# All sums of gated values and of down weights on VectorE, and twelve load tiles in the FFN stages of a hybrid decoder layer

## The chip, the cores and the metric

The kernel runs on one core of a Trainium2 chip. Its engines are TensorE (PE, with its weight loads shown apart as PEld), VectorE (DVE), ScalarE (ACT), GpSimd (POOL) and SyncE (SP). In this kernel SP issues the transfers between the chip's main memory and the on-chip tiles. The metric is the time of one execution on the device in microseconds (us); the median of several runs is compared.

## The reference, cut to what matters

One layer of a decoder trunk over 2048 tokens of width 1024, in fp32:

```python
u = rmsnorm(h, attn_pre_norm); proj = u @ w_in
o_hg = rmsnorm(hgrn2_mix(...)) * silu(hg)          # gated linear recurrence, 4 heads
o_sb = rmsnorm(stick_breaking_mix(sq, sk, sv))     # attention, 8 heads of width 64
h = h + rmsnorm(concat(o_hg, o_sb) @ w_out, attn_post_norm)
u = rmsnorm(h, ffn_pre_norm)
gate, up = split(u @ w_gate_up, 2816)              # w_gate_up: 1024 x 5632
y = (silu(gate) * up) @ w_down                     # w_down: 2816 x 1024
h = h + rmsnorm(y, ffn_post_norm)
out = h + (p @ ple_proj) * sigmoid(h @ ple_gate)   # ple_gate: 1024 x 1024
```

The change concerns the third block, the FFN: the products with w_gate_up and w_down and what lies between them.

## The kernel before

**Products.** Every fp32 product is made of three matmuls on rounded parts (function mm3, lines 223 to 225): an operand is split into a high part, a copy that ACT makes (line 811), and a low part, operand minus high part, which DVE or POOL computes (line 812, in pair_of). Tiles are 128 x 512 fp32 values, 256 KB.

**Seven products instead of eight.** The FFN and the PLE gate multiply 2 x 2 blocks by the scheme of Strassen and Winograd: seven products, in the order CHAIN = (1, 2, 6, 3, 7, 5, 4), of blocks and of sums of blocks. Each product's result leaves PSUM through DVE or ACT in the function chain, which adds it to the others (lines 816 and 819 are the helpers sub and add; line 926 is ACT's copy of the first product).

**Stages.** The tokens stand in four groups of 512, taken two at a time. After attention and the output projection come six stages, put in a row by the class Drive: gate_up(0), down(0), gate_up(1), down(1), ple(0), ple(1). gate_up has 11 blocks of the 2816 columns, seven steps each. A step has two parts: prepare, which loads and splits its weights, and run, which issues its 24 matmuls (two banks of 12 each). Drive calls prepare three steps ahead of run in a gate_up stage, four ahead in a down stage and five in a ple stage.

**Between gate/up and down.** When a block's last product is done, run applies the gate (sigmoid on ACT, line 996; products on DVE, lines 997 and 998) and holds four quarters of gated values: h11, h12, h21, h22. down needs seven operands of them: h11, h12, h22 and the four sums s1 to s4. They are computed in tiles named hs (lines 1013, 1014, 1018, 1019) and stored to hid_s in main memory (lines 1016 and 1021); down loads them back from there. The hs tiles come from a pool "acc" that the gate's sg tiles and the transposer's results share.

**Sums of down weights.** down also needs four sums of the w_down blocks for each of its 11 column blocks k. down_combos(k) loads four blocks, forms four sums in place (b_combos, four instructions of line 816) and stores them to wd_s (line 834). It is called while gate_up(0) runs, once every six steps from step 12 on. Even k have their sums on DVE, odd k on POOL. ple_combos does the same for the PLE gate's weights during gate_up(1).

**Other work in gate_up(0).** Also hung on its steps: the operands of its later products (t_second, four loads of u_s for each k), the late normalization of the last token group (post_late: DVE line 715, POOL line 716, ACT line 718) and the transposition of two groups (turn: loads at line 730, transposes on TensorE at line 745, copies on ACT at line 751, stores at line 752).

**Load tiles.** All these loads (function load, line 796) and the transposer's go into tiles named wr, of which there are WR = 10; a load can start when the instructions that read the tile's last contents are done. SP issues loads and stores in one queue, in order.

**Order.** TensorE's instructions stand in the order of the program (manual_schedule for PE alone). Those of the other engines and of SP are put in order by a planner that simulates the program's time; changing an instruction's engine can change its place and that of others. Each engine then executes its queue in order.

Of the kernel before, what the change touches and what calls it, by code (L numbers as in the profile page):

```python
# [25 lines left out]
DFF = 2816  # L26
PLE = 256
EPS = 1e-6
WR = 10
LEVELS = (1, 2, 4, 8, 16, 32, 64)  # L30
BL = 32

# [56 lines left out]
def hybrid_block(  # L89
# [89 lines left out]
    def mm_bank():  # L179
        mm_count[0] += 1  # L180
        return bank(mm_tags[mm_count[0] % len(mm_tags)])
# [8 lines left out]
    def xt(name="xt"):  # L190
        return fb.tile([P, GT], F32, tag="xt", name=name, bufs=8)
# [30 lines left out]
    def mm3(o, l, r, start, stop):  # L222
        nc.tensor.matmul(o, l[0], r[0], start=start, stop=False)  # L223
        nc.tensor.matmul(o, l[0], r[1], start=False, stop=False)  # L224
        nc.tensor.matmul(o, l[1], r[0], start=False, stop=stop)  # L225
# [559 lines left out]

    SLOTS = {"u": (12, 16), "w": (4, 4), "wr": (WR, 0), "acc": (2, 4)}
    big = [None, None]
# [6 lines left out]
    def load(src, shape=None):  # L794
        r = slot("wr", 0, "wr")
        nc.sync.dma_start(r if shape is None else shape(r), src)
        return r

    def acc(name="acc"):
        turns["acc"] += 1  # L800
        return slot("acc", 0 if turns["acc"] % 3 == 0 else 1, name)

    def pair_of(src, kind, prod, lo_engine):
        if kind == "u":
            side = 0 if prod in (1, 2, 6) else 1
        else:
            turns["w"] += 1
            side = turns["w"] % 2
        hi = slot(kind + "h", side, kind + "h", F32R)
        lo = slot(kind + "l", side, kind + "l", F32R)  # L810
        nc.scalar.copy(hi, src)  # L811
        lo_engine.tensor_tensor(lo, src, hi.bitcast(F32), op=ALU.subtract)  # L812
        return hi, lo

    def sub(e, o, a, b):
        e.tensor_tensor(o, a, b, op=ALU.subtract)

    def add(e, o, a, b):
        e.tensor_tensor(o, a, b, op=ALU.add)  # L819

    V, G = nc.vector, nc.gpsimd

    def b_combos(b11, b12, b21, b22, e):

        sub(e, b11, b12, b11)
        sub(e, b12, b22, b12)
        sub(e, b22, b22, b11)
        sub(e, b21, b22, b21)

    def combos(blk, dst, e):  # L830
        t = [load(blk(i, j)) for i, j in ((0, 0), (0, 1), (1, 0), (1, 1))]
        b_combos(*t, e)
        for i, r in zip((1, 3, 4, 2), t):
            nc.sync.dma_start(dst[i - 1], r)

    wd_s = [dram.tile([4, P, GT], F32, tag=f"wd_s{k}", name=f"wd_s{k}") for k in range(DFF // 256)]
    wp_s = [dram.tile([4, P, GT], F32, tag=f"wp_s{k}", name=f"wp_s{k}") for k in range(ND // 2)]

    def down_combos(k):
        def blk(i, j):  # L840
            r = (2 * k + i) * P
            return w_down[r:r + P, j * GT:(j + 1) * GT]

        combos(blk, wd_s[k], G if k % 2 else V)

    def ple_combos(k):
        def blk(i, j):
# [74 lines left out]
    def chain(prod, c, b, new):  # L922

        if prod == 1:
            c["u"] = new("cu")
            nc.scalar.copy(c["u"], b)
        elif prod == 2:
            c[1, 1] = new("c11")
            add(V, c[1, 1], b, c["u"])
        elif prod == 6:  # L930
            add(V, c["u"], b, c["u"])
        elif prod == 3:
            c[1, 2] = new("c12")
            add(V, c[1, 2], b, c["u"])
        elif prod == 7:
            add(V, c["u"], b, c["u"])
        elif prod == 5:
            add(V, c[1, 2], b, c[1, 2])
            c[2, 2] = new("c22")
            add(V, c[2, 2], b, c["u"])  # L940
        else:
            c[2, 1] = c["u"]
            sub(V, c[2, 1], c["u"], b)
# [9 lines left out]
    def gate_up(grp, tt):  # L953
        def block(fb):
            s = {}
            cs = [{}, {}]

            def wload(i, j):
                out = []
                for n in range(2):  # L960
                    r = slice((4 * j + 2 * n) * P, (4 * j + 2 * n + 2) * P)
                    c0 = i * DFF + fb * 256
                    out.append(load(w_gate_up[r, c0:c0 + 256].rearrange("(k p) n -> p k n", p=P),
                                    lambda r: r.rearrange("p (k n) -> p k n", k=2)))
                return out

            def prepare(prod):
                if prod == 1:
                    w = wload(0, 0)
                elif prod == 2:  # L970
                    w = wload(0, 1)
                elif prod == 6:
                    w, a21, a22 = wload(0, 0), wload(1, 0), wload(1, 1)
                    s["s1"] = [xt("s1") for _ in range(2)]
                    s["s3"] = [xt("s3") for _ in range(2)]
                    for n in range(2):
                        add(V, s["s1"][n], a21[n], a22[n])
                        sub(V, s["s3"][n], w[n], a21[n])
                        sub(V, w[n], s["s1"][n], w[n])
                    s["s2"] = w  # L980
                elif prod == 3:
                    w = wload(0, 1)
                    for n in range(2):
                        sub(V, w[n], w[n], s["s2"][n])
                elif prod == 7:
                    w = s["s3"]
                elif prod == 5:
                    w = s["s1"]
                else:
                    w = wload(1, 1)  # L990
                s[prod] = [pair_of(t, "w", prod, V if n or prod in (6, 3) else G) for n, t in enumerate(w)]

            def gated(j):
                for q in range(2):
                    sg = acc("sg")
                    nc.scalar.activation(sg, cs[q][1, j], AF.Sigmoid)
                    nc.vector.tensor_tensor(sg, cs[q][1, j], sg, op=ALU.mult)
                    nc.vector.tensor_tensor(cs[q][2, j], cs[q][2, j], sg, op=ALU.mult)

            def run(prod):  # L1000
                for q in range(2):
                    b = mm_bank()
                    for k in range(ND // 2):
                        o = (k % 2) * 256 + q * P
                        mm3(b, [t[:, o:o + P] for t in s[prod][k // 2]], tt[prod, k], k == 0, k == ND // 2 - 1)
                    chain(prod, cs[q], b, new_gu)
                if prod == 5:
                    gated(2)
                if prod == 4:
                    gated(1)  # L1010
                    h11, h12, h21, h22 = cs[0][2, 1], cs[1][2, 1], cs[0][2, 2], cs[1][2, 2]
                    s1, s3 = acc("hs"), acc("hs")
                    add(G, s1, h21, h22)
                    sub(G, s3, h11, h21)
                    for i, t in ((1, h11), (2, h12), (4, h22), (5, s1), (7, s3)):
                        nc.sync.dma_start(hid_s[grp][fb, i - 1], t)
                    s2, s4 = acc("hs"), acc("hs")
                    sub(G, s2, s1, h11)
                    sub(G, s4, h12, s2)
                    for i, t in ((6, s2), (3, s4)):  # L1020
                        nc.sync.dma_start(hid_s[grp][fb, i - 1], t)

            return {prod: (lambda p=prod: prepare(p), lambda p=prod: run(p)) for prod in CHAIN}

        blocks = [block(fb) for fb in range(DFF // 256)]
        steps = []
        if grp == 0:
            for part in (CHAIN[:3], CHAIN[3:]):
                for b in blocks[:2]:
                    steps += [b[p] for p in part]  # L1030
            blocks = blocks[2:]
        return steps + [b[p] for b in blocks for p in CHAIN]
# [269 lines left out]
    for k in range(DFF // 256):  # L1302
        at(0, 12 + 6 * k - (k > 9), lambda k=k: down_combos(k))
# [45 lines left out]
```

## Time and profile before

| | |
|---|---|
| median of 3 runs | 3080.39 us (3078.42 to 3082.84) |
| profiled execution | 3079.93 us, of it 3078.1 us in the span of the profile |
| TensorE busy | 2928.8 us, 95% of the span |
| DVE, POOL, ACT busy | 2042.8, 1603.7, 1580.6 us |
| mean granted TensorE clock | 0.987 |
| transfers | 602.29 MB, mean 196 GB/s |

Times in the rows shown below count from the start of the span. A row of an instruction has its start, its duration, the engine, the line, the operation, the tiles written and read with their shapes, the count, and in brackets the idle time of the engine before it and what ended that idle time. A row of a wait names who waited for whom, then the total in us, the number of waits and the longest. Matmuls overlap, so the distance from one start to the next says more than a duration. The granted clock is given as a share of full speed.

### The profile page before, as it was taken

Reading aid. Unit: us, or ns where it says so; the run is one execution under the profiler, and the core shown is the slowest. Engines: PE = TensorE matmul, PEld = TensorE weight load, DVE = VectorE, ACT = ScalarE, POOL = GpSimd, SP = SyncE. Lnnn points to the kernel's source line nnn. Section 1 sums busy time; section 2 is a strip of 40 time slices with the busy share of each in tenths; the row PEclk is TensorE's granted clock in tenths of the full one; section 3 lists DMA queues with packets and bytes.
Section 4 is the critical chain, followed back from the end, with each engine's and each line's share of the span. In section 5 each row is a group of like instructions: output and inputs, shape, how many; then the busy total and the mean of one; then the engine's idle time right before and its main releaser. Section 6 shows DMA issues by size and latency. Waiting matters only on the chain. (4 is left out here: it accounts for less than half of the span.)

```text
span 3078.1 us, 52969 instructions
## 1 busy us (share of the span) xinstructions
PE 2928.8 (95%) x18280; PEld 2429.9 (79%) x18280; DVE 2042.8 (66%) x2809; ACT 1580.6 (51%) x3188; POOL 1603.7 (52%) x1598
## 2 busy tenths in 40 slices
PE   8999999999999998888998999999899999999989
PEld 7888787878787877778776877788788888887767
DVE  3556566677767776745877766856687766656674
ACT  5666656666667666757523233445432323545442
POOL 3344455545556666857454544645634343556564
PEclk9999999999999999999999999999999999999999
DMA  7765565555444443457767767766955555677874
GB/s 216 217 211 164 157 185 158 148 156 162 141 140 150 147 144 122 164 176 264 253 212 245 238 214 236 234 198 218 328 179 171 172 170 175 209 225 251 286 246 144
DMA packets 469421, 602.29 MB, mean 196 GB/s; under 512 B 43168, under 2 KB 277664, under 8 KB 469152
## 3 DMA queue, kind: packets, MB, share of 16 engines
q1 hardware_dynamic: 469152, 598.91, 61.4%
q8 instruction: 144, 2.36, 0.3%
q14 instruction: 125, 1.02, 0.1%
HBM read 439.89 MB, written 158.86 MB: 195 GB/s over the span
## 5 line engine op out<-in xcount | busy, mean ns | idle before, releaser
L811 ACT CAST wh<-wr 128x512 fp32r<-128x512 f32 x600 | 352.3, 618 | 511.1 <-PE mm L224 139.0
L812 POOL TENSOR_TENSOR wl<-wr,wh 128x512 fp32r<-128x512 f32 x256 | 368.7, 1447 | 386.3 <-ACT wh L811 366.8
L435 POOL TENSOR_TENSOR a<-be,ring 128x512 f32<-128x512 f32 (+2 forms) x320 | 318.4, 995 | 434.5 <-DVE ring L431 418.3
L223 PE MATMUL mm<-uh,wh 128*128 128x512 f32 x1168 | 484.5, 415 | 5.2 <-DVE vv L350 3.2
L225 PE MATMUL mm<-uh,wl 128*128 128x512 f32 x1168 | 460.6, 394 | 0.0
L224 PE MATMUL mm<-ul,wh 128*128 128x512 f32 x1168 | 459.0, 393 | 1.6 <-DVE ul L812 1.6
L812 DVE TENSOR_TENSOR wl<-wr,wh 128x512 fp32r<-128x512 f32 x344 | 308.9, 902 | 204.4 <-ACT wh L811 177.6
L431 DVE TENSOR_TENSOR_SCAN ring<-z,ring,be 128x512 f32<-128x512 f32 x192 | 245.6, 1279 | 113.4 <-ACT z L417 110.0
L223 PE MATMUL mm<-wh,uh 128*128 128x256 f32 (+1 forms) x992 | 308.6, 311 | 0.0
L224 PE MATMUL mm<-wl,uh 128*128 128x256 f32 (+1 forms) x992 | 293.4, 296 | 1.6 <-DVE wl L812 1.3
L225 PE MATMUL mm<-wh,ul 128*128 128x256 f32 (+1 forms) x992 | 292.9, 295 | 0.0
L225 PEld LDWEIGHTS mm<-uh,wl 128*128 128x128 f32 x1168 | 220.5, 189 | 51.0
L223 PEld LDWEIGHTS mm<-uh,wh 128*128 128x128 f32 x1168 | 221.4, 190 | 47.6 <-issue 3.3
L224 PEld LDWEIGHTS mm<-ul,wh 128*128 128x128 f32 x1168 | 221.9, 190 | 41.7 <-DVE ul L812 2.0
L448 DVE TENSOR_TENSOR al<-tr,ah 128x512 fp32r<-128x512 f32 (+1 forms) x320 | 192.0, 600 | 90.1 <-ACT ah L446 89.4
L209 ACT CAST wh<-wr 128x512 fp32r<-128x512 f32 x288 | 178.2, 619 | 135.8 <-PE mm L224 81.5
L210 POOL TENSOR_TENSOR wl<-wr,wh 128x512 fp32r<-128x512 f32 x144 | 189.1, 1313 | 98.2 <-ACT wh L209 95.0
L446 ACT CAST ah<-tr 128x512 fp32r<-128x512 f32 (+1 forms) x320 | 167.6, 524 | 110.1 <-PE tr L443 107.1
L416 ACT ACTIVATE be<-z 128x512 f32<-128x512 f32 (+2 forms) x320 | 171.0, 534 | 90.5 <-PE z L410 38.3
L224 PEld LDWEIGHTS mm<-wl,uh 128*128 128x128 f32 x992 | 191.3, 193 | 8.0 <-DVE wl L812 1.7
L223 PEld LDWEIGHTS mm<-wh,uh 128*128 128x128 f32 x992 | 191.0, 193 | 8.1
L225 PEld LDWEIGHTS mm<-wh,ul 128*128 128x128 f32 x992 | 190.7, 192 | 4.3
(305 smaller groups left out, 7285.6 us busy)
## 6 DMA issues: line engine op xcount, KB each, us to landing
wr<-in_w_gate_up_dram SPq DMA_DIRECT2D x308, 256.0 KB, 3.4
wr<-in_w_in_dram SPq DMA_DIRECT2D x224, 256.0 KB, 3.1
wr<-hid_s SPq DMA_DIRECT2D x154, 256.0 KB, 3.1
wr<-in_w_down_dram SPq DMA_DIRECT2D x110, 256.0 KB, 3.3
hid_s<-hs SPq DMA_DIRECT2D x88, 256.0 KB, 2.7
wr<-wd_s SPq DMA_DIRECT2D x88, 256.0 KB, 3.1
kt<-k_s SPq DMA_DIRECT2D x80, 256.0 KB, 3.1
vt<-v_s SPq DMA_DIRECT2D x80, 256.0 KB, 3.3
```

Source lines behind the costliest of these rows:

```text
L209: nc.scalar.copy(hi, src)
L210: (lo_engine or nc.gpsimd).tensor_tensor(lo, src, hi.bitcast(F32), op=ALU.subtract)
L223: nc.tensor.matmul(o, l[0], r[0], start=start, stop=False)
L224: nc.tensor.matmul(o, l[0], r[1], start=False, stop=False)
L225: nc.tensor.matmul(o, l[1], r[0], start=False, stop=stop)
L416: nc.scalar.activation(be[:, :n], z[:, :n], AF.Sigmoid, scale=0.125)
L431: nc.vector.tensor_tensor_scan(r[:, o:o + n][:, ::-1], z[:, :n][:, ::-1], be[:, :n][:, ::-1], init, op0=ALU.mult, op1=ALU.bypass)
L435: nc.gpsimd.tensor_tensor(a[:, :n], be[:, :n], r[:, o + 1:o + n + 1], op=ALU.mult)
L446: nc.scalar.copy(hi[:, lo_c:], tr[:, lo_c:])
L448: nc.vector.tensor_tensor(lo[:, lo_c:], tr[:, lo_c:], hi[:, lo_c:].bitcast(F32), op=ALU.subtract)
L811: nc.scalar.copy(hi, src)
L812: lo_engine.tensor_tensor(lo, src, hi.bitcast(F32), op=ALU.subtract)
```

## The change

Three things: the four sums of gated values in every gate/up block are DVE's instead of POOL's (88 instructions in the two stages); the four sums of w_down for odd k are DVE's as for even k (20 instructions); and the pool of load tiles of the FFN and PLE stages has 12 tiles instead of ten, 4 KB more in each partition. The PLE gate's sums stay as they are.

```diff
-WR = 10
+WR = 12
...
-        combos(blk, wd_s[k], G if k % 2 else V)
+        combos(blk, wd_s[k], V)
...
                     s1, s3 = acc("hs"), acc("hs")
-                    add(G, s1, h21, h22)
-                    sub(G, s3, h11, h21)
+                    add(V, s1, h21, h22)
+                    sub(V, s3, h11, h21)
                     for i, t in ((1, h11), (2, h12), (4, h22), (5, s1), (7, s3)):
                         nc.sync.dma_start(hid_s[grp][fb, i - 1], t)
                     s2, s4 = acc("hs"), acc("hs")
-                    sub(G, s2, s1, h11)
-                    sub(G, s4, h12, s2)
+                    sub(V, s2, s1, h11)
+                    sub(V, s4, h12, s2)
                     for i, t in ((6, s2), (3, s4)):
                         nc.sync.dma_start(hid_s[grp][fb, i - 1], t)
```

V is VectorE (nc.vector), G is GpSimd (nc.gpsimd).

## The prediction, made before the changed kernel was run

> **What bounds the kernel now.** I read the page first, then busy time by stage, then what TensorE waited for, then the instructions around its longest waits.
>
> ```profile
> span 3078.1 us, 52969 instructions
> ...
> PE 2928.8 (95%) x18280; PEld 2429.9 (79%) x18280; DVE 2042.8 (66%) x2809; ACT 1580.6 (51%) x3188; POOL 1603.7 (52%) x1598
> ```
>
> TensorE is the bound: 95% of the span. No other engine passes 66%, so the change can only move the 5% in which TensorE stands still, and what a low clock adds. The profiled execution took 3079.93 us (its span and 1.8 us around it), the median of the runs is 3080.39; the sum below is made against 3079.9.
>
> The FFN load tiles come into use shortly before 1486 us. Stages from there (columns: stretch and its length, then busy us of each engine, granted clock, share of the DMA engines, GB/s):
>
> ```profile
> 1486.00:1560.00 74.00, 66.51 (x288) 53.57 (x289) 68.06 (x90) 29.93 (x57) 31.58 (x29) 0.93 0.64 208
> 1560.00:1930.00 370.00, 349.06 (x1524) 282.43 (x1523) 259.28 (x367) 116.87 (x221) 170.32 (x119) 0.98 0.69 228
> ...
> 2196.00:2640.00 444.00, 438.36 (x1921) 357.48 (x1922) 330.19 (x444) 144.35 (x245) 179.69 (x120) 0.99 0.58 187
> ...
> 2860.00:3079.00 219.00, 200.02 (x853) 158.70 (x851) 129.96 (x164) 77.60 (x137) 115.31 (x82) 0.97 0.63 216
> ```
>
> The first two rows are the gate/up stage of group 0: TensorE misses 7.5 and 20.9 us of 444. The third is the same stage of group 1, which misses 5.6, at its start. What it waited for, in 1486 to 1930 and then from 1930 on:
>
> ```profile
> PE hg L745 <- ACT acc L751: 19.1, 6, 12.4
> PE av L225 <- DVE wl L812: 4.7, 2, 4.2
> ```
>
> ```profile
> PE z L224 <- POOL wl L812: 4.0, 1, 4.0
> PE tr L225 <- DVE wl L812: 3.9, 1, 3.9
> PE mm L223 <- ACT wh L811: 3.7, 1, 3.7
> ```
>
> Nobody on TensorE waits for a sum that is moved. What the change can do comes indirectly: through when DVE and POOL get to other work, and through when loads start. The longest wait, followed back through the instructions:
>
> ```profile
> 1655.60 0.75 DVE L715 SCALAR_TENSOR_TENSOR wr<-wr,row_scales 128x512 f32<-128x512 f32 x1 [1.31 <-DMA wr<-in_attn_post_norm_dram]
> ...
> 1661.63 6.57 SPq L796 DMA_DIRECT2D wr<-in_w_gate_up_dram  x4
> 1665.88 0.69 DVE L819 TENSOR_TENSOR s<-wr 128x512 f32<-128x512 f32 x1 [3.73 <-DMA wr<-in_w_gate_up_dram]
> ...
> 1677.11 1.41 POOL L816 TENSOR_TENSOR wr<-wr 128x512 f32<-128x512 f32 x1 [16.70 <-DMA wr<-in_w_down_dram]
> 1677.31 1.75 DVE L715 SCALAR_TENSOR_TENSOR wr<-wr,row_scales 128x512 f32<-128x512 f32 x1
> ...
> 1680.15 1.71 POOL L716 TENSOR_TENSOR wr<-wr 128x512 f32<-128x512 f32 x1
> 1680.66 1.75 DVE L998 TENSOR_TENSOR c<-c,sg 128x512 f32<-128x512 f32 x1
> ...
> 1681.89 0.63 ACT L718 ACTIVATE junk<-wr 128x512 bf16<-128x512 f32 x1 [3.44 <-POOL wr L716]
> ...
> 1683.55 0.68 ACT L751 ACTIVATE acc<-hg,g_ffn 128x512 f32<-128x512 f32 x1
> ...
> 1684.28 1.12 PE L745 MATMUL hg<-ident,wr 128*128 128x128 f32 x4 [12.36 <-ACT acc L751]
> ```
>
> (The first row is an earlier L715, alone: 0.75.) Read it upwards: the transpose waits for ACT's copy (L751), which stands behind ACT L718, which waits for POOL L716, which waits for DVE L715 and stood behind a w_down sum (L816) on POOL; L715 stood in a row of DVE work that began only when a gate/up load landed at 1665.9, and SP needed 6.6 us to issue those four loads. Late loads are at the root, with a POOL sum of the kind that is moved in between.
>
> The start of the stage is of the same kind, before any moved sum is due (the first is after 1560):
>
> ```profile
> 1520.94 0.62 ACT L811 CAST uh<-wr 128x512 fp32r<-128x512 f32 x1 [1.86 <-DMA wr<-u_s]
> 1521.01 1.29 DVE L816 TENSOR_TENSOR wr<-wr 128x512 f32<-128x512 f32 x2 [0.76 <-DMA wr<-u_s]
> ...
> 1522.22 1.76 DVE L812 TENSOR_TENSOR wl<-wr,wh 128x512 fp32r<-128x512 f32 x1
> ...
> 1524.03 0.79 PE L225 MATMUL av<-uh,wl 128*128 128x512 f32 x1 [4.18 <-DVE wl L812]
> ```
>
> **The change, part by part.** Rows of the groups that it touches (POOL first, then DVE; last columns: busy, mean ns of one, idle before):
>
> ```profile
> L816 POOL TENSOR_TENSOR wr<-wr 128x512 f32<-128x512 f32 x28 | 39.3, 1403 | 63.2 <-DMA wr<-in_w_down_dram 44.9 <-DVE c L998 11.4 <-DVE wr L816 4.9
> L816 POOL TENSOR_TENSOR hs<-cu,c 128x512 f32<-128x512 f32 x22 | 38.9, 1768 | 23.1 <-DVE cu L998 21.9 <-DMA wr<-in_w_down_dram 1.2
> L819 POOL TENSOR_TENSOR hs<-c,c 128x512 f32<-128x512 f32 x22 | 36.9, 1677 | 133.4 <-DVE c L998 81.2 <-issue 38.1 <-DMA wr<-in_w_gate_up_dram 14.1
> L816 POOL TENSOR_TENSOR hs<-hs,cu 128x512 f32<-128x512 f32 x22 | 36.2, 1646 | 0.2
> ...
> L816 POOL TENSOR_TENSOR hs<-cu,hs 128x512 f32<-128x512 f32 x22 | 32.3, 1469 | 1.1 <-PE av L225 0.7
> ```
>
> ```profile
> L812 DVE TENSOR_TENSOR wl<-wr,wh 128x512 fp32r<-128x512 f32 x342 | 306.2, 900 | 204.4 <-ACT wh L811 177.6 <-DMA wr<-hid_s 16.7 <-PE z L224 5.2
> ...
> L998 DVE TENSOR_TENSOR cu<-cu,sg 128x512 f32<-128x512 f32 x44 | 49.5, 1130 | 0.1
> ```
>
> Moved: 88 gated sums (4 in each of 22 blocks) and 20 sums of w_down (5 odd k of 4; the other 8 of the 28 are the PLE gate's and stay). POOL loses 38.9 + 36.9 + 36.2 + 32.3 + 20 x 1.403 = 172 us. DVE gains 108 x 0.69 (the s<-wr instruction at 1665.88, alone) = 74.5 us.
>
> But POOL's sums stretch DVE's: at 1680.66, beside POOL L716, an instruction of this form took 1.75 instead of 0.69. So each moved sum gives DVE back between 0 (nothing beside it) and 1.06 us. The group cu<-cu,sg, which runs as the gated sums begin, has an excess of 0.44 each (19.4 us over 88 sums, 0.22 per sum); wl<-wr,wh has 72 us in all. I take 0.4, since more than one group is stretched by the same sum. Net: 108 x 0.29 = +31 us of DVE.
>
> Is DVE then the bound? In group 0's stage it had 68.1 + 259.3 = 327 of 444; 64 of the sums fall there: 327 + 64 x 0.29 = 346 (78%), without relief 371 (84%). In group 1's: 330 + 44 x 0.29 = 343 (77%), without relief 361 (81%). Both lie under TensorE's busy time, so the moved work costs 0 on the path; TensorE's products hide it. With that cover gone altogether it would cost the whole 74.5 us.
>
> SP issues the same transfers in both kernels. A block's four sums take 6.6 us in a row on POOL (144.3 / 22) and 2.8 on DVE, so the hid_s stores, and the loads queued behind them on SP, can go up to 3.8 us sooner; I count that as a margin, since stores were no wait of TensorE.
>
> **Two more load tiles.** A load starts when a tile is free.
>
> ```profile
> wr<-in_w_gate_up_dram SPq DMA_DIRECT2D x144, 256.0 KB, 3.5
> wr<-in_w_down_dram SPq DMA_DIRECT2D x44, 256.0 KB, 3.4
> ```
>
> In the 444 us these two kinds alone make 188 loads, one per 2.4 us, so two tiles bring a load forward by 0 (where its place in SP's order holds it) to 4.7 us. I take 3, as the waits above begin at a load and other loads share the tiles. What that returns:
>
> - Start of the stage (4.18 and some 1 us of waits, then slow matmuls): 3 us of the wait and 2 of the slow stretch, together 5; bounds 0 and 11 (7.5 missed and 3.5 at half clock).
> - The 12.36 us: 3 for the load, 1.0 for L715 (1.75 against 0.75 alone), 1.1 because POOL L716 no longer stands behind the w_down sum after L715 ended at 1679.06, less 0.7 for a sum that now runs on DVE ahead of it, and 0.6 of the slow stretch: 5; bounds 0 and 14.5.
> - The other five transposes that waited (19.1 - 12.4 = 6.7): 1.5.
> - Start of group 1's stage (3.9 and the slow stretch behind it): 3; bounds 0 and 6.2.
> - PLE, 3.7 + 4.0 behind loads: 2; bounds 0 and 7.7.
>
> Sum 16.5: 3079.9 - 16.5 = 3063.4, forecast **3063**.
>
> The slow stretches, behind the start's wait, the 12.36 and the 3.9:
>
> ```profile
> 1524.00:1531.00 7.00, 6.40 (x14) 4.62 (x15) 7.00 (x8) 4.31 (x8) 4.12 (x3) 0.50 0.54 171
> ...
> 1684.00:1691.00 7.00, 6.72 (x24) 5.52 (x25) 6.51 (x7) 1.15 (x3) 7.00 (x6) 0.70 0.98 334
> ...
> 2199.00:2206.00 7.00, 6.27 (x20) 4.70 (x19) 7.00 (x9) 0.59 (x1) 4.26 (x3) 0.67 0.86 256
> ```
>
> They lose 7 x 0.50 = 3.5, 2.1 and 2.3 us. [...]
>
> **Rivals.**
>
> ```profile
> POOL wr L816 <- DMA wr<-in_w_down_dram: 44.9, 3, 24.8
> ```
>
> ```profile
> 1516.85 0.39 PE L224 MATMUL mm<-ul,wh 128*128 128x512 f32 x1
> 1517.08 0.39 PE L225 MATMUL mm<-uh,wl 128*128 128x512 f32 x1
> ```
>
> *DVE is held at the head of its queue (slower).* The w_down sums on POOL waited for their loads 44.9 us in three waits, the longest 24.8, the one above 16.70, with little behind them there. On DVE the same wait holds the evacuations of PSUM and the splits for the next products. gate_up prepares three products ahead; one takes 24 matmuls, which start 0.23 us apart, 5.5 us. If two of the three are really ready, TensorE runs 11 us without DVE; waits of 24.8 and 16.7 then cost 13.8 + 5.7 = 19.5, and slow stretches of 3.5 and 2.1: 25 us. Less the 5 + 3 + 2 that come elsewhere: 3095. It decides from a wait of about 11 us on DVE ahead of a moved sum. For it: the 1665.88 row, where a 3.73 us wait held all of DVE. Against: DVE already carries the even k's sums, the loads come earlier with 12 tiles, and where the sums stand in DVE's order is planned anew. [...]
>
> *No change.* SP issues in a planned order; if its place in that order, not a tile, holds a load, the lead is 0. The chain through ACT L718 and L751 stays. 3079. For it: no moved sum is waited for by TensorE, and group 1's stage lost nothing after its start with ten tiles.
>
> *All of it goes.* Every miss of group 0's stage (28.4 and 5.6 of slow clock) and of group 1's start (6.2): 3080 - 40 = 3040. Against: the chain of L745 runs through ACT's order, which stays long.
>
> **How the numbers follow.** Forecast 0.48 (its own range 3050 to 3074), all gone 0.12 (3040), no change 0.18 (3079), DVE held 0.22 (3095). About 0.2% (6 us) is what a measurement here tells from no change. Faster 0.48 + 0.12 = 0.60, within 0.2% 0.18, slower 0.22. The range takes in the no-change case and most of the two outer ones: 3038 to 3094.
>
> **What would show it.** Right: no hs sum and no w_down sum on POOL, POOL's busy time down by some 170 us, DVE's up by 20 to 45 and not by 75 (relief), wl<-wr,wh nearer 800 ns than 900; DVE's and ACT's waits for gate/up loads fewer in 1486 to 1930; the 4.18 and 12.36 us waits shorter. Wrong: DVE waiting over 11 us for w_down with TensorE idle behind it; DVE over 90% in a gate/up stage; the same waits at L745 with loads no earlier; or a new wait in the PLE stage, since every queue but TensorE's may be ordered anew.

## The result and the profile after

The changed kernel took 3061.07 us in the median of six runs (3057.24 to 3070.8), the kernel before 3079.4 in six runs beside it (3073.11 to 3082.84): a ratio of 0.9945 with a 95% interval of 0.9927 to 0.9963, so 0.55% faster. The forecast was 3063. The profiled execution took 3057.24 us, 3055.5 of it in the span.

The page of the kernel after, span and busy times:

```profile
span 3055.5 us, 52953 instructions
...
PE 2920.4 (96%) x18280; PEld 2425.4 (79%) x18280; DVE 2065.6 (68%) x2917; ACT 1583.7 (52%) x3188; POOL 1463.9 (48%) x1490
```

TensorE issues the same 18280 matmuls and, busy for 96% of the span, is still the bound. DVE has 108 instructions more and only 22.8 us more of busy time; POOL has 108 fewer and loses 139.8 us.

The stages of the kernel after, with the same columns as before (stretch, length, busy us of PE, PEld, DVE, ACT and POOL, granted clock, DMA share, GB/s):

```profile
1486.00:1560.00 74.00, 69.41 (x304) 56.30 (x303) 68.24 (x93) 31.00 (x59) 34.56 (x29) 0.95 0.69 221
1560.00:1930.00 370.00, 353.67 (x1545) 287.53 (x1545) 296.14 (x440) 123.15 (x227) 98.38 (x65) 0.98 0.73 239
1486.00:1930.00 444.00, 423.08 (x1848) 343.82 (x1847) 364.39 (x532) 154.15 (x286) 132.94 (x93) 0.97 0.72 236
2196.00:2640.00 444.00, 441.75 (x1940) 360.45 (x1939) 332.93 (x488) 151.54 (x258) 125.35 (x76) 1.00 0.58 189
```

In the first 444 us after 1486 TensorE does 36 matmuls more than before (1848 against 288 + 1524 = 1812). At 0.23 us from one start to the next (1516.85 to 1517.08 in the kernel before) that is 8.3 us. DVE is at 364 of 444, 82%.

What TensorE waited for in the kernel after, first in group 0's gate/up stage, then from 1930 on (whom it waited for, total us, times, longest):

```profile
PE hg L745 <- ACT acc L751: 13.1, 2, 10.3
PE av L225 <- DVE wl L812: 4.6, 2, 2.5
PE z L223 <- DVE cu L816: 2.9, 1, 2.9
```

```profile
PE mm L224 <- POOL wl L812: 6.7, 1, 6.7
...
PE mm L225 <- DVE wl L812: 2.2, 2, 1.9
```

The long wait at L745 is 10.3 instead of 12.4, the five smaller ones have become one of 2.8 (13.1 less 10.3), the 3.9 at the start of group 1's stage is gone, and a wait of 6.7 in the PLE stage is new. The wait of 2.9 for a sum of products on DVE was 1.3 before.

TensorE's order is the same in every kernel here, so the i-th matmul of one can be set against the i-th of another. Adding up how much sooner each comes than before gives the gain by place. One execution of each kernel stands behind this table, and the part ahead of the FFN, where nothing is changed, differs by up to 9 us between executions, so the column is shown too:

| us gained against before | ahead of the FFN | gate_up(0) | everything after it |
|---|---|---|---|
| after | 1.7 | 9.2 | 12.0 |
| twelve tiles alone | -8.6 | -5.9 | 7.7 |
| all sums on DVE, ten tiles | -0.3 | 17.8 | 3.1 |

The second and third rows are the first two experiments below. They already show the split: the sums gain in gate_up(0), the tiles lose there and gain later (the profiled execution of the second row is a long one, with a span of 3086.2 us, most of it lost ahead of the FFN). The difference between the first and the third row, 8.6 us less in gate_up(0) and 8.9 more after it, says the same of the tiles. So do the other two pairs of kernels that differ in the tiles alone (with one set of sums moved, below): with twelve tiles they gain 3.6 and 2.7 us less in gate_up(0), and 5.7 and 5.4 more after it.

### The profile page after: what moved, and what is told of

It is laid out like the page before. It is cut to its first block, busy times and chain, and to the rows that moved or that the text cites. A ratio compares the mean times of both kernels' runs of the same rounds, so it can differ in the third digit from the quotient of the medians.

```text
span 3055.5 us, 52953 instructions
## 1 busy us (share of the span) xinstructions
PE 2920.4 (96%) x18280; PEld 2425.4 (79%) x18280; DVE 2065.6 (68%) x2917; ACT 1583.7 (52%) x3188; POOL 1463.9 (48%) x1490
## 4 chain that ended last, share of the span: by engine, by line
PE 41%; DMA 6%; DVE 5%; POOL 3%; issue 3%; ACT 1%; SPq 0%; POOLq 0%; ACTq 0%; DVEq 0%
PE mm L223 6%; PE mm L224 6%; PE mm L225 6%; PE z L225 4%; PE z L223 4%; PE z L224 4%; PE tr L223 2%; PE tr L224 2%; PE tr L225 2%; PE av L225 2%; PE av L224 2%; PE av L223 2%; DMA wr<-in_w_gate_up_dram 1%; DVE wr L816 1%; DMA wr<-in_ffn_post_norm_dram 1%
## 5 line engine op out<-in xcount | busy, mean ns | idle before, releaser
L225 PE MATMUL mm<-uh,wl 128*128 128x512 f32 x1168 | 458.9, 393 | 0.0
L812 DVE TENSOR_TENSOR wl<-wr,wh 128x512 fp32r<-128x512 f32 x344 | 299.2, 877 | 181.8 <-ACT wh L811 166.1
L225 PE MATMUL mm<-wh,ul 128*128 128x256 f32 (+1 forms) x992 | 293.6, 296 | 0.0
L225 PEld LDWEIGHTS mm<-uh,wl 128*128 128x128 f32 x1168 | 219.4, 188 | 50.6
L812 POOL TENSOR_TENSOR wl<-s,wh 128x512 fp32r<-128x512 f32 x44 | 97.0, 2211 | 270.8 <-ACT wh L811 242.0
L224 PEld LDWEIGHTS mm<-wl,uh 128*128 128x128 f32 x992 | 191.9, 193 | 12.2 <-POOL wl L812 7.1
```

## The experiments

Every kernel was timed against the kernel before on the same chip; a ratio below 1 is faster than before. The kernel before was timed anew in each of four groups (3079.4, 3079.78, 3079.62 and 3081.08 us); its first median is shown.

| kernel | load tiles | sums on DVE | median us | ratio, 95% interval |
|---|---|---|---|---|
| before | 10 | none of the moved ones | 3079.4 | 1 |
| e1_tiles | 12 | none | 3075.13 | 0.9983 [0.9972, 0.9994] |
| e5_hs | 10 | gated | 3065.27 | 0.9958 [0.9944, 0.9973] |
| e6_wd | 10 | w_down | 3067.6 | 0.9958 [0.9944, 0.9972] |
| e2_sums | 10 | both | 3061.47 | 0.9941 [0.9925, 0.9957] |
| e3_tiles_hs | 12 | gated | 3057.98 | 0.9926 [0.9912, 0.9941] |
| e4_tiles_wd | 12 | w_down | 3066.2 | 0.9949 [0.9933, 0.9965] |
| after | 12 | both | 3061.07 | 0.9945 [0.9927, 0.9963] |
| e8_late_tiles | 10, then 12 | both | 3062.0 | 0.9934 [0.9917, 0.995] |
| e7_no_hs | 10 | w_down; gated left out | 3058.91 | 0.9931 [0.9915, 0.9948] |
| e9_own_out | 10, two for the transposer | both | 3059.94 | 0.9941 [0.9924, 0.9958] |
| e10_copy_dve | 10 | both | 3068.51 | 0.9961 [0.9946, 0.9976] |
| e11_late_copy | 10, then 12 | both | 3070.92 | 0.9961 [0.9947, 0.9976] |
| e12_after_copy | 12 | both | 3059.34 | 0.993 [0.9915, 0.9944] |

### The two halves of the change

Twelve tiles alone:

```diff
-WR = 10
+WR = 12
```

> Twelve load tiles alone, all sums where they were before. Theory A (the gain of 18 us is loads that start earlier): 3060 to 3068, with the waits of 1840 to 1930 and at the start of group 1's gate/up stage gone or halved as in the changed kernel. Theory B (the gain comes from the sums: DVE no longer stretched by them, and the stores and the acc tiles free sooner): 3075 to 3083, with those waits still there. Theory C (only the planner's new order matters, and any small edit moves the time by some 10 us either way): no relation to the changed kernel's stalls, place by place.

All sums on DVE, ten tiles:

```diff
-        combos(blk, wd_s[k], G if k % 2 else V)
+        combos(blk, wd_s[k], V)
...
-                    add(G, s1, h21, h22)
-                    sub(G, s3, h11, h21)
+                    add(V, s1, h21, h22)
+                    sub(V, s3, h11, h21)
...
-                    sub(G, s2, s1, h11)
-                    sub(G, s4, h12, s2)
+                    sub(V, s2, s1, h11)
+                    sub(V, s4, h12, s2)
```

> All 108 sums on DVE, ten load tiles. Theory A: 3075 to 3083, DVE's busy time up by some 25 us and TensorE's waits as before. Theory B: 3060 to 3068. If the two parts need one another: both this run and the one with the tiles alone stay above 3070.

The tiles alone bring 0.17% (by the ratio 0.0017 x 3079.4 = 5 us); the sums alone bring 0.59% (18 us), as much as the whole change. The intervals are far apart. With ten tiles the sums bring the whole gain. Neither theory of the first expectation holds whole: the time of e1_tiles lies in Theory B's range, but the waits between 1840 and 1930 and at the start of group 1's stage are gone, as Theory A had it.

Twelve tiles alone, in group 0's gate/up stage: busy times of the stage, what TensorE waited for, and the instructions around the two long waits (start, duration, engine, line; the bracket is the idle time before and what ended it):

```profile
1486.00:1930.00 444.00, 411.84 (x1813) 335.80 (x1812) 335.58 (x448) 146.99 (x279) 210.96 (x148) 0.96 0.70 228
```

```profile
PE hg L745 <- ACT acc L751: 19.1, 2, 11.4
PE av L223 <- DVE c L819: 4.7, 1, 4.7
PE z L225 <- DVE wl L812: 3.7, 1, 3.7
```

```profile
1632.28 1.15 ACT L996 ACTIVATE sg<-c 128x512 f32<-128x512 f32 x2 [14.73 <-DVE c L819]
...
1637.81 0.67 ACT L751 ACTIVATE acc<-hg,g_ffn 128x512 f32<-128x512 f32 x1
...
1638.53 1.12 PE L745 MATMUL hg<-ident,wr 128*128 128x128 f32 x4 [7.63 <-ACT acc L751]
...
1696.00 2.35 DVE L998 TENSOR_TENSOR cu<-cu,sg 128x512 f32<-128x512 f32 x2
1697.78 0.69 ACT L751 ACTIVATE acc<-hg,g_ffn 128x512 f32<-128x512 f32 x1 [7.78 <-DVE cu L998]
...
1698.52 1.11 PE L745 MATMUL hg<-ident,wr 128*128 128x128 f32 x4 [11.44 <-ACT acc L751]
```

TensorE is busy for 411.8 us of the window, before for 66.51 + 349.06 = 415.6; this execution reaches the stage some 10 us later, so the window takes in a little more of the work ahead of it. The waits at L745 sum to the same 19.1 us as before, in two instead of six. In the first, ACT's copy L751 stands in ACT's queue behind a sigmoid L996 that itself waited 14.7 us for its operand; in the second it waits 7.8 us for DVE's L998, which reads an sg tile of the pool "acc" and so releases the tile that the copy writes. Neither ends with a load. More of ACT's idle time in this stage now lies ahead of a sigmoid. The row of ACT's waits for it, of before, of twelve tiles alone, and of the changed kernel:

```profile
ACT sg L996 <- DVE c L819: 51.3, 14, 13.7
```

```profile
ACT sg L996 <- DVE c L819: 102.8, 18, 18.4
```

```profile
ACT sg L996 <- DVE c L819: 88.9, 21, 15.8
```

In the five kernels with twelve tiles in this stage it is 79 to 103 us, in eight of the nine with ten 48 to 64. The ninth, e7_no_hs, has 78.1 and the largest gain of all in this stage (24.6 us, table below), so this idle time alone does not make a kernel slow; that ACT's order is what twelve tiles cost here is argued, not shown.

All sums on DVE with ten tiles, the same views:

```profile
1486.00:1930.00 444.00, 430.30 (x1887) 350.60 (x1886) 369.62 (x538) 155.74 (x290) 134.11 (x95) 0.98 0.72 239
```

```profile
PE hg L745 <- ACT acc L751: 7.2, 1, 7.2
PE av L225 <- DVE wl L812: 4.0, 2, 3.4
```

```profile
1661.52 0.69 DVE L819 TENSOR_TENSOR s<-wr 128x512 f32<-128x512 f32 x1 [3.23 <-DMA wr<-in_w_gate_up_dram]
...
1673.68 0.74 DVE L715 SCALAR_TENSOR_TENSOR wr<-wr,row_scales 128x512 f32<-128x512 f32 x1
...
1674.56 1.59 POOL L716 TENSOR_TENSOR wr<-wr 128x512 f32<-128x512 f32 x1 [1.95 <-DVE wr L715]
...
1676.18 0.63 ACT L718 ACTIVATE junk<-wr 128x512 bf16<-128x512 f32 x1 [1.36 <-POOL wr L716]
...
1677.83 0.68 ACT L751 ACTIVATE acc<-hg,g_ffn 128x512 f32<-128x512 f32 x1
...
1678.57 1.11 PE L745 MATMUL hg<-ident,wr 128*128 128x128 f32 x4 [7.18 <-ACT acc L751]
```

This is the chain of before (L715, L716, L718, L751, L745) with the POOL sums taken out of it: L715 takes 0.74 us instead of 1.75, and POOL is idle and waits for L715 instead of standing behind its own work. From L715 to L745 it takes 4.9 us instead of 7.0. That is 2.1 of the 5.7 us by which the transpose comes sooner, less 0.7 because DVE's row from the load to L715 is longer (12.2 us for 11.4). The other 4.4 us come from further up: the row of DVE work still begins when a gate/up load lands, but that is at 1661.5 instead of 1665.9, with no tile more. SP's queue shows where the load was held. Before, and then with all sums on DVE:

```profile
1640.34 3.37 SPq L1021 DMA_DIRECT2D hid_s<-hs  x2
...
1646.34 0.40 SPq L796 DMA_DIRECT2D wr<-in_w_gate_up_dram  x1
```

```profile
1640.46 0.32 SPq L1021 DMA_DIRECT2D hid_s<-hs  x1
...
1642.08 0.39 SPq L796 DMA_DIRECT2D wr<-in_w_gate_up_dram  x1
```

Before, POOL ends the block's last gated sum at 1643.4; its store to hid_s, and the stores of w_down sums behind it, hold SP, and the next gate/up load is issued at 1646.3. With the sums on DVE the last one ends at 1640.4, and the load is issued 4.3 us sooner, while TensorE is only 0.1 us ahead at this place. TensorE does 1887 matmuls in the stretch instead of 1812: 75 x 0.23 = 17 us.

### Which sums

Each of these keeps one of the two sets of sums on POOL; the edit is the part of the diff above for the other set. With twelve tiles, gated sums on DVE, then w_down's sums on DVE:

```diff
-WR = 10
+WR = 12
...
-                    add(G, s1, h21, h22)
+                    add(V, s1, h21, h22)
```

> Twelve tiles and the 88 gated sums on DVE, the odd k's w_down sums left on POOL. Theory A: 3058 to 3068, as the changed kernel. Theory B: between 3060 and 3070, by the share of the gated sums (88 of 108). If the w_down sums on POOL make the chain over POOL L716 and ACT L718 to the transposer late: over 3068, with a wait of over 10 us at L745 that goes through them.

```diff
-WR = 10
+WR = 12
...
-        combos(blk, wd_s[k], G if k % 2 else V)
+        combos(blk, wd_s[k], V)
```

> Twelve tiles and the 20 w_down sums of odd k on DVE, the gated sums left on POOL. Theory A: 3060 to 3068. Theory B: 3070 to 3078, since most sums stay on POOL. The rival of the prediction (DVE held at a w_down sum) would show as a DVE wait over 11 us for w_down and a time over 3080.

With ten tiles, the same two:

> The 88 gated sums alone on DVE, ten tiles, w_down sums of odd k on POOL. If it is the gated sums that bring the gain of all sums (18 us): 3058 to 3066. If it is the w_down sums, which held POOL L716 and with it ACT behind their loads: 3074 to 3081. If each brings its part: 3064 to 3073.

> The 20 w_down sums of odd k alone on DVE, ten tiles, gated sums on POOL. The same three cases: 3074 to 3081, 3060 to 3067, 3064 to 3073. In the first of them the three waits of POOL for w_down loads (44.9 us before) are gone and TensorE is no better for it.

With ten tiles the gated sums bring 13 us and the w_down sums 13 (0.42% each by the ratios) and both 18. With 4 to 5 us either way on each, this is not told from a plain addition; the 20 w_down sums bring about as much as the 88 gated ones. So a share by number, which Theory B took for e4_tiles_wd, does not fit: its 3066.2 lies outside the range of 3070 to 3078. The time of e5_hs lies in two of the ranges and does not decide between them; e6_wd's fits "each brings its part". e3_tiles_hs came out just under the ranges of both its theories. With twelve tiles the gated sums alone are at least as good as both (3058.0 and 3061.1, the intervals overlap). No difference between e3_tiles_hs, e2_sums and the changed kernel can be told; none of the kernels is shown to beat it.

What the tiles are worth depends on what else is moved. Beside the gated sums they bring 10 us (0.9958 to 0.9926, intervals that do not overlap), alone 5, beside the w_down sums 3 and beside both none, the last two not told from nothing. Why they help beside the gated sums and not beside both was not followed up.

The two sets shorten the long wait at L745 in different ways. With the gated sums alone on DVE, and then the w_down sums alone, both with ten tiles:

```profile
PE hg L745 <- ACT acc L751: 11.9, 4, 8.8
```

```profile
PE hg L745 <- ACT acc L751: 15.4, 4, 10.7
```

The wait of 12.4 us gets 3.6 us shorter with the gated sums, 1.7 with the w_down sums and 5.2 with both. Counted against TensorE's place, matmul by matmul, the DVE addition that begins the row (1665.88 before) comes 3.6, 0.4 and 3.9 us sooner. With the gated sums alone L715 still takes 1.76 us and POOL still does a w_down sum just ahead; with the w_down sums alone both are as in e2_sums. So the gated sums bring the load forward, and the w_down sums clear the chain behind it.

### What the moved work costs

The gated sums are left out, and the stores take the gated values in their place:

```diff
-                    s1, s3 = acc("hs"), acc("hs")
-                    add(V, s1, h21, h22)
-                    sub(V, s3, h11, h21)
-                    for i, t in ((1, h11), (2, h12), (4, h22), (5, s1), (7, s3)):
...
+                    for i, t in ((1, h11), (2, h12), (4, h22), (5, h21), (7, h21), (6, h12), (3, h12)):
```

> As the kernel with all sums on DVE and ten tiles, but the 88 gated sums are left out: the four sums are not computed, and the stores take h21 and h12 in their place (as many stores of the same size, another output). If the moved work is hidden on DVE: 3057 to 3064, as with the sums (3061). If DVE's place in the chain still costs time: 10 us or more under it, at most 27 us (88 x 0.3, the net DVE time per sum in the prediction).

Against e2_sums this takes 88 instructions off DVE and 2.6 us off the time (3061.47 to 3058.91), which the intervals (0.9925 to 0.9957 and 0.9915 to 0.9948) do not tell from nothing, while DVE's busy time falls by 64.6 us (2060.2 to 1995.6). The moved sums are covered by TensorE's products, or very nearly. The edit also takes the hs tiles out of the pool "acc", and in the profile gate_up(0) gains 6.8 us more than in e2_sums; how the two share in that is not separated.

### Tiles only where they help

By the table of gains, twelve tiles lose in gate_up(0) and gain later. So two of the twelve come into use only from down(0) on: every sixth load goes to them.

```diff
-    SLOTS = {"u": (12, 16), "w": (4, 4), "wr": (WR, 0), "acc": (2, 4)}
+    SLOTS = {"u": (12, 16), "w": (4, 4), "wr": (WR, 0), "wx": (2, 0), "acc": (2, 4)}
+    late = [False, 0]
...
+    def wr():
+        late[1] += late[0]
+        return slot("wx" if late[0] and late[1] % 6 == 0 else "wr", 0, "wr")
```

> All sums on DVE; ten load tiles in group 0's gate/up stage and twelve from the first step of down(0) on (every sixth load then goes to one of two extra tiles). Reading so far: twelve tiles cost some 8 us in group 0's gate/up stage and return some 10 us later, at the start of group 1's stage, behind down(1) and in PLE. If that holds: 3050 to 3057. If the loss and the gain are only two sides of another planned order: 3058 to 3066.

It gains 16.9 us in gate_up(0), like ten tiles (17.8), but only 5.6 after it, not 12; the time, 3062.0, is that of the two it was to beat, as the second case of the expectation had it. Two separate tiles in a fixed turn are not the same as a pool of twelve, and the later gain of the profiles did not add up.

### The hold at the transposer's copy

Four kernels go after what is left at L745. The transposer's results get two tiles of their own instead of the shared pool:

```diff
-        return turn(src, dst, gain, "hg", wr, acc, scales)
+        return turn(src, dst, gain, "hg", wr, lambda: slot("te", 0, "te"), scales)
```

> All sums on DVE, ten load tiles, and the transposer of group 0's gate/up stage copies into two tiles of its own instead of the six that the gate and the gated sums share. If the 7.2 us wait at L745 that is left with the sums on DVE stands for a shared tile: it goes, 3050 to 3056. If it stands in ACT's order behind L718 (which waits for POOL L716 and DVE L715): it stays, 3057 to 3065.

The copies L751 are made on DVE instead of ACT, with ten tiles, with ten and later twelve, and in the changed kernel:

```diff
+                elif on_dve:
+                    nc.vector.tensor_scalar(e, b, gain[:, k:k + 1], None, op0=ALU.mult)
...
-        return turn(src, dst, gain, "hg", wr, acc, scales)
+        return turn(src, dst, gain, "hg", wr, acc, scales, on_dve=True)
```

> All sums on DVE, ten load tiles, and the transposer's 16 copies out of PSUM (L751) on DVE instead of ACT. If the 7.2 us wait is ACT's order: it goes or falls under 3 us, 3050 to 3056. If it is a shared tile or DVE's own order: it stays, 3058 to 3066.

> Ten load tiles in group 0's gate/up stage and twelve later, all sums and the transposer's copies on DVE: what the runs so far point to as the best of these. If both parts keep what they bring alone: 3046 to 3054 and faster than the changed kernel (3061). If every such step only makes another order of about the same worth: 3055 to 3063.

> The changed kernel (all sums on DVE, twelve tiles) with the transposer's copies on DVE. Its waits at L745 (2.8 and 10.3 us) end with a copy that stood behind the gate's sigmoid on ACT and then for a tile that DVE L998 had to free. If ACT's order is what twelve tiles cost in this stage: 3045 to 3053. If the tile is: little, 3056 to 3062.

With tiles of their own the waits at L745 disappear from the stage, and gate_up(0) gains 21.9 us in the profile; but what comes after it gains only 0.8, and the ratio (0.9941) is that of e2_sums. The wait went as the first case of the expectation had it, and the time (3059.94) stayed in the range of the second: what it brought in this stage was not seen in the whole. With the copy on DVE the wait grows. In e10_copy_dve, TensorE's waits and DVE's instructions ahead of the copy:

```profile
PE hg L745 <- issue: 15.5, 1, 15.5
```

```profile
1674.01 0.68 DVE L821 TENSOR_TENSOR hs<-c,c 128x512 f32<-128x512 f32 x1
...
1681.08 0.68 DVE L818 TENSOR_TENSOR hs<-cu,hs 128x512 f32<-128x512 f32 x1
1681.69 0.74 DVE L751 TENSOR_SCALAR acc<-hg,g_ffn 128x512 f32<-128x512 f32 x1
```

The copy now stands behind a dense row of DVE work with the moved sums in it, and TensorE waits 15.5 us. The profile names no releaser for this wait ("issue"); the transpose starts at 1682.53, 0.1 us after the copy's end. (The edit adds two lines, so L818 and L821 are the helpers sub and add.) e11_late_copy has the same (15.2), e12_after_copy 11.2 and 3.5. In medians the first is 7 us slower than e2_sums, with overlapping intervals; the last is not told from the changed kernel. The first two came out above every range of their expectations, the third in the range of its second case. Moving the copy to DVE did not free it; in DVE's order too it has work ahead of it.

Over the eleven kernels whose copy stays on ACT, the sum of the waits at L745 goes with the gain in gate_up(0), both from one profile of each:

| kernel | waits at L745, us | gate_up(0), us gained |
|---|---|---|
| before | 19.1 | 0 |
| e1_tiles | 19.1 | -5.9 |
| e6_wd | 15.4 | 9.8 |
| e3_tiles_hs | 14.3 | 9.6 |
| after | 13.1 | 9.2 |
| e5_hs | 11.9 | 13.2 |
| e4_tiles_wd | 8.0 | 7.1 |
| e8_late_tiles | 7.4 | 16.9 |
| e2_sums | 7.2 | 17.8 |
| e9_own_out | 0 | 21.9 |
| e7_no_hs | 0 | 24.6 |

Broadly, fewer waits go with more gain. The two kernels without such waits gain most; e1_tiles and e4_tiles_wd, which have other waits (4.7 and 3.7 us, and 6.8 for DVE at L225), gain less than their rows would say, and the three kernels between 13.1 and 15.4 us gain about the same. Removing 19.1 us of waits comes with 22 to 25 us, more than the waits themselves; the mean granted clock of the stage is 0.99 and 1.00 in the last two rows and 0.97 before.

## Why the prediction was right, and where it was not

**The total.** 3063 was forecast, 3061.07 came. The sum made against the profiled execution was 16.5 us; the medians differ by 18.3. The sum came out right by luck, as the part on the tiles shows.

**TensorE as the bound, and the cover.** Right. The moved work lies under TensorE's products: leaving the gated sums out returns 2.6 us in the medians, not their 88 x 0.69 = 61. In group 0's stage DVE is at 364 of 444 us, where 346 was forecast with relief and 371 without; in group 1's at 332.9, where 343 was forecast.

**DVE's and POOL's busy time.** DVE rose by 22.8 us, inside the 20 to 45 forecast and far from 75: the relief per moved sum is (74.5 - 22.8) / 108 = 0.48 us, where 0.4 was taken. But this rise holds the tiles' part as well: e1_tiles, where no sum is moved, has 21.6 us more than before (2064.4), and e2_sums, with ten tiles, 17.4 (2060.2), a relief of 0.53. What the tiles' other order adds to DVE's time the prediction put at nothing. The relief did not fall where it was looked for. Groups from the FFN stages, DVE's and POOL's, of before and then of after (columns: busy, mean ns of one, idle before):

```profile
L812 DVE TENSOR_TENSOR wl<-s,wh 128x512 fp32r<-128x512 f32 x44 | 51.3, 1168 | 6.1 <-ACT wh L811 6.0
L819 DVE TENSOR_TENSOR c<-mm,cu 128x512 f32<-128x512 f32 x74 | 50.0, 681 | 24.7 <-PE mm L225 24.5
...
L812 POOL TENSOR_TENSOR wl<-s,wh 128x512 fp32r<-128x512 f32 x44 | 70.6, 1607 | 41.3 <-ACT wh L811 40.5 <-DMA hid_s<-hs 0.8
```

```profile
L812 DVE TENSOR_TENSOR wl<-wr,wh 128x512 fp32r<-128x512 f32 x342 | 296.5, 874 | 181.8 <-ACT wh L811 166.1 <-PE z L224 6.3 <-DMA wr<-hid_s 4.2
...
L819 DVE TENSOR_TENSOR c<-mm,cu 128x512 f32<-128x512 f32 x74 | 49.9, 681 | 22.8 <-PE mm L225 22.6
...
L812 DVE TENSOR_TENSOR wl<-s,wh 128x512 fp32r<-128x512 f32 x44 | 33.6, 763 | 2.9 <-ACT wh L811 2.9
L998 DVE TENSOR_TENSOR cu<-cu,sg 128x512 f32<-128x512 f32 x44 | 31.9, 730 | 0.0
...
L812 POOL TENSOR_TENSOR wl<-s,wh 128x512 fp32r<-128x512 f32 x44 | 97.0, 2211 | 270.8 <-ACT wh L811 242.0 <-DVE hs L819 16.2 <-DMA wd_s<-wr 7.2
```

The group wl<-wr,wh went from 900 to 874 ns, not to near 800; cu<-cu,sg (1130 to 730) and wl<-s,wh (1168 to 763) gave back 17.6 and 17.7 us. These ran beside the gated sums: in the kernel before, of those that have a timeline row of their own, 30 of 40 and 18 of 42 overlap one on POOL. POOL fell by 139.8 us and not by 172, for the most part because its own wl<-s,wh got 26.4 us longer (70.6 to 97.0), now beside a denser DVE (busy for 364 us of group 0's stage instead of 327). The prediction counted the stretch in one direction only.

**The two more load tiles.** This is the step that failed: "What that returns", the bullets that book the lead of 3 us as gain, and among them the two on the transposes. Apart from the 1.4 us that the second bullet gives to L715, L716 and the sum moved ahead of them (1.0 + 1.1 - 0.7), the whole 16.5 was the tiles'. The tiles alone measured 5 us, and beside both sets of sums nothing that can be told from zero (3061.47 and 3061.07). The lead itself came: ACT's waits for gate/up loads in group 0's stage fell from 35.9 us to 9.4 with the tiles alone and to 0.7 in the changed kernel (DVE's, 35.0 before, are 44.5 and 32.9), and the load that DVE awaits at 1665.9 came 7.0 us sooner in both, counted against TensorE's place, where at most 4.7 was worked out. At the starts of the two gate/up stages it returned about what was booked or more. Between them, where the transposes wait, it did not: from 1559 to 1838 the aligned matmuls lose 19.1 us with the tiles alone and 4.0 in the changed kernel, and gain 7.9 with the sums alone.

The second failing term is the one put at nothing. That the hid_s stores, "and the loads queued behind them on SP, can go up to 3.8 us sooner" was written down and then counted "as a margin, since stores were no wait of TensorE". With all sums on DVE and ten tiles the load behind those stores was issued 4.3 us sooner, and 3.6 us of the long wait went with the gated sums alone. The sums measured 18 us, where the prediction gave them 1.4. Two errors of nearly one size stood against each other.

- *Start of the stage, 5.* Nearly so, and the tiles' own: in the 74 us from 1486 the kernel after does 304 matmuls where before did 288 (16 x 0.23 = 3.7 us), and the aligned matmuls gain 4.1 us there, 4.0 in e1_tiles, 0.8 in e2_sums. The long wait did not get shorter in sum (2.5 and 2.1 us in place of 4.2). Two smaller waits went (1.0 and 1.6 us), and the stretch at a granted clock of 0.50 is some 3.4 us shorter (1520.8 to 1527.6 after, 1521.0 to 1531.2 before), worth 1.7.
- *The 12.36 us, 5.* It became 10.3 with the tiles and sums, 11.4 with tiles alone, 7.2 with the sums alone. The links named were the right ones (L715 stretched, L716 behind POOL's own work, a late load ahead of both), and the 1.0 + 1.1 - 0.7 is what e2_sums shows from the load to the transpose (2.1 - 0.7). What failed is that a sooner load ends the wait: with twelve tiles the wait is ended by something else. In the kernel after:

```profile
1664.24 1.62 POOL L716 TENSOR_TENSOR wr<-wr 128x512 f32<-128x512 f32 x1 [14.82 <-DVE wr L715]
...
1676.11 0.68 DVE L998 TENSOR_TENSOR c<-c,sg 128x512 f32<-128x512 f32 x1
...
1676.72 1.28 DVE L998 TENSOR_TENSOR cu<-cu,sg 128x512 f32<-128x512 f32 x2
1677.43 0.69 ACT L751 ACTIVATE acc<-hg,g_ffn 128x512 f32<-128x512 f32 x1 [5.68 <-DVE cu L998]
...
1678.17 1.11 PE L745 MATMUL hg<-ident,wr 128*128 128x128 f32 x4 [10.31 <-ACT acc L751]
```

  L716 is done 11.6 us ahead of the copy, and 12 us sooner than before against TensorE's place, in e1_tiles too; the copy waits, by its releaser, for a tile of the shared pool until DVE's L998, which stands late in DVE's row. A wait that is taken away at one link is held by the next: this the prediction allowed for, but it did not look at who else uses the transposer's pool.
- *The other five transposes, 1.5.* Too small. Three of them, 5.7 us, lay between 1838 and 1939; the aligned matmuls gain 9.1 us in that part, in e1_tiles and e2_sums as well as in the changed kernel. Either half of the change removed them (one set of sums alone, with ten tiles, gains 5.4 or 4.5 there).
- *Start of group 1's stage, 3; PLE, 2.* The first was right and too small: the wait of 3.9 is gone and the matmuls around it (2190 to 2210 in the kernel before) gain 8.3 us, over the bound of 6.2; a wait of 1.4 just ahead of it went too. e1_tiles gains the same 8.3, e2_sums 2.7 with the wait at 1.8. In the PLE stage the waits of 3.7 and 4.0 went, but one of 6.7 came, the "new wait in the PLE stage" that the prediction named as a sign against it; the stage still gains 2.3 us in this profile. The wait comes with the tiles: e1_tiles has 6.7 there too, e3_tiles_hs 6.6, e2_sums at most 2.9.

**DVE held at the head of its queue.** Not seen. DVE's waits for w_down loads in group 0's stage after the change:

```profile
DVE wr L816 <- DMA wr<-in_w_down_dram: 9.0, 8, 2.4
```

On POOL they had been 44.9 us, up to 24.8 at once; on DVE, which had 10.4 for the even k alone, they are no more than before, the longest 2.4, far from the 11 from which it would decide. The order was planned anew, so this does not show what a held DVE would cost. What work that stands late in DVE's queue can cost is seen elsewhere: with L751 behind the sums in e10_copy_dve, TensorE waits 15.5 us.

**The clock behind the waits.** The windows of seven us behind the start of group 0's stage, behind the place at the start of group 1's where the wait of 3.9 was, and behind the new PLE wait, in the kernel after:

```profile
1524.00:1531.00 7.00, 7.00 (x24) 5.53 (x24) 7.00 (x7) 3.46 (x7) 6.70 (x4) 0.74 0.54 154
2182.00:2189.00 7.00, 6.23 (x33) 5.02 (x32) 7.00 (x8) 1.52 (x3) 5.75 (x4) 1.00 1.00 320
2948.00:2955.00 7.00, 6.67 (x17) 5.27 (x18) 1.82 (x2) 1.66 (x4) 7.00 (x6) 0.54 0.96 339
```

With the wait gone the clock stays whole (1.00 for 0.67); with waits of 2.5 and 2.1 it is 0.74 for 0.50; behind 6.7 us it is 0.54. The 0.74 is a mean: the clock is 0.50 from 1521 to 1527 and 1.00 from 1528 on, where before it was 0.50 until 1531. In the kernel after no single wait there was longer than 2.5 us. TensorE was busy for 2.9 of the 7 us from 1516, and the two short waits close together went with the same 0.50 as the one of 4.18 before, for 6.8 us instead of 10.2. So the first stretch did not come back whole when its longest wait became shorter. From what wait on the clock falls, and whether single waits or their sum decide, these profiles do not show.

**What stays open.** Why an order planned with twelve tiles puts sigmoids ahead of the copies in gate_up(0) was not isolated. Every edit reorders the queues of DVE, ACT, POOL and SP at many places, and no kernel here keeps an order while it changes the tiles alone. For the longest wait the sums' part is taken apart above; how much of their 18 us in all is loads issued sooner, how much the freed POOL queue, how much the shorter DVE instructions, and how much the acc tiles that come free sooner (2.8 us of sums on DVE for 6.6 on POOL, if alone) is not separated; that e9_own_out is not faster than e2_sums speaks against a large part for the last. Own tiles for the transposer together with twelve load tiles were not tried.

## What to carry to other kernels

When a change has two parts, give each its own price before adding: here a total that came out right to 2 us hid one part that added nothing measurable to the other. Moving short additions off a slower engine (the 88 gated sums took 1.64 us each on POOL before and 0.82 on DVE after) paid here, 18 us with ten tiles, though nobody on the bounding engine waits for them: through the chains in which that engine is a link, and through the stores of their results, behind which loads stand in one queue (the load at 1646.3 was issued 4.3 us sooner). So follow the longest waits link by link, ask of each link what frees it, and do not put such a term at nothing because it is itself no wait. A larger buffer pool is also a new order for every planned queue; judge it by what ends the waits afterwards, and look at all pools on that chain, not only the one that is enlarged.

## What was not expected of the hardware

In these profiles the stretch of SBUF additions goes both ways. Where POOL's sums went, DVE's gate products with two SBUF operands (cu<-cu,sg) fell from 1130 to 730 ns, and POOL's remaining splits (wl<-s,wh) beside a denser DVE rose from 1607 to 2211 ns, while DVE additions with one operand in PSUM (c<-mm,cu) stayed at 681 ns in both kernels. In the kernel before, in the timeline's single rows from 1486 to 2660, cu<-cu,sg took 1.23 us on average where POOL was busy for over 0.3 of its time (34) and 0.68 elsewhere (6), and c<-mm,cu 0.68 in both cases (28 and 23). What holds these instructions no profile here shows. With ten tiles in both kernels, 108 additions moved from POOL to DVE raised DVE's busy time by 17.4 us instead of 74.5, and lowered POOL's by 148.7 (1603.7 to 1455.0) instead of 172. One profile of each stands behind these figures, and they move with the order: with twelve tiles in both, DVE's rise is 1.2 us (2064.4 to 2065.6).
